# Small products of a one-block encoder: full-height filter products, f32r norm sums and first transform back, the low rank in one run, and GLA's values ahead of q and k

## The chip, the cores and the metric

The kernel runs on one core of a Trainium2 chip. The core has a matrix engine (TensorE, here PE), a vector engine (VectorE, DVE), a scalar engine (ScalarE, ACT), a general one (GpSimd, POOL), and SyncE (SP), which here issues DMAs; each executes its own instructions in order and waits for others on semaphores. The metric is the device time of one execution in microseconds, as the median of several. Lower is better.

## The reference

One encoder block on 256 rows of width 2048, in fp32. `w_in` projects the normed input to the operands of four mixers of width 512 each; their outputs go through `w_out`; cross attention over 256 memory rows and a SwiGLU follow.

```python
h = rms_norm(x, norm_g[l, 0])
q, k, v, g, lr, u_f, u_h, u_s = jnp.split(h @ w_in[l], split_at, axis=-1)
y_a = gla_mixer(q, k, v, g, lr, ...)        # gated linear attention, 4 heads, gates from lr (rank 2 x 16)
y_b = rms_norm(fnet_mixer(u_f), grp_norm_g[l, 0])
filt = hyena_filters(feats, w1, b1, w2, b2, w3, freq, decay)
y_c = rms_norm(hyena_mixer(u_h, hy_conv_w[l], filt, hy_skip[l]), grp_norm_g[l, 1])
y_d = rms_norm(shortconv_mixer(u_s, sc_conv_w[l]), grp_norm_g[l, 2])
x = x + concatenate([y_a, y_b, y_c, y_d]) @ w_out[l]
x = x + cross_attention(rms_norm(x, norm_g[l, 1]), mem_n, w_xq[l], w_xkv[l], w_xo[l])
x = x + swiglu(rms_norm(x, norm_g[l, 2]), w_gate_up[l], w_down[l])

def hyena_filters(...):      # an MLP of 64 over position features, twice sin, then:
    h = h @ w3               # 64 -> 2 orders x 2 directions x 512
    h = h * exp(-t * abs(decay))
    return rfft(two_sided(h))
def long_conv(z, filt, skip):
    return irfft(rfft(z, n=2 * seq) * filt)[:, :seq] + z * skip
def hyena_mixer(u, conv_w, filt, skip):
    v, x1, x2 = split(short_conv(u, conv_w))
    z = x1 * long_conv(v, filt[0], skip[0])
    return x2 * long_conv(z, filt[1], skip[1])
```

## The kernel before

**Large products.** All weights come as one stream of 128x128 blocks in the order of use. SP loads slabs of 16 blocks into three `raw` buffers (L83); ACT casts half a slab, eight blocks, to f32r (`wh`, L104) and DVE subtracts that from the original (`wl`, L105), two or three halves ahead of their use. Activations are split in the same way into slots of 128x512: 256 columns of high part, 256 of low. A product of two fp32 numbers is three f32r products. In `gemm` a block is the stationary operand: one matmul of `wh` with 512 columns (L301) and one of `wl` with 256 (L302), or three of 256 where it is `narrow` (L298, L299, L302). In `gemm_rows` the activations are stationary and four blocks pass through as 512 columns, three matmuls for each half of the rows (L346 to L348).

**Order.** The large products follow each other without a gap: keys (`w_xkv`, L301, from 5 us), the attention's values (L346 to L348, from 99 us), then `w_in`: Hyena's operands and GLA's k and q (L301, from 203 us), GLA's values (L346 to L348, from 303 us), the first three short convolution products and Fnet's (narrow, from 329 us), the other short convolution products (from 371 us), GLA's gate (narrow, from 443 us), then `w_out` (from 469 us) and what follows.

**Small work.** Generators in the class `Background` issue the small products, norms and transforms between those matmuls. `poll` lets a generator go on when the PE time counted since its last `yield` is over 1.3 us (or what the yield asks for) and little DVE work is owed. Tile's scheduling then sets the place within an engine's order. PE executes in order, so a small product whose operand is late holds up the large ones behind it.

**The places that the change touches.**

- `Hyena.filters`, L1033 and L1034: filters as `hs` (128 rows: 64 of the high part of the hidden layer, 64 of its low part) times `wh`, then the upper 64 rows times the upper 64 of `wl`. The weight rows are loaded twice, one copy above the other.
- `Hyena.dft`, L979 to L981: the transform forward, as three f32r products for each parity. `Hyena.convs`, L1100: the first transform back, two fp32 products for each parity from the table `tab`, which holds a factor of 1/256. L1119: the second transform back, also fp32.
- `rstd_bank`, L276 to L278: a diagonal of the reciprocal norms (DVE) times a matrix of ones (fp32), which spreads the norm of each row over all partitions; called once for the memory, once for x, for three group norms and for four GLA heads. `rstd_end` copies the result out (L283).
- `start_x`, L430 to L441: during the last value product it scales each of 16 tiles of x and splits it; after every fourth it issues four fp32 products of 32 columns each (L438), side by side in PE's columns, which add up to GLA's low rank `lr`.
- `Gla.open`: loads the gate weights `gkw` to a tile of their own.

Of the kernel before, what the change touches and what calls it, by code (L numbers as in the profile page):

```python
# [13 lines left out]
F32 = mybir.dt.float32  # L14
F32R = mybir.dt.float32r
# [22 lines left out]

ROWS = ((256, 512), (768, 832), (NBLK - 48 * FT, NBLK))

# [127 lines left out]
class Block:  # L168
# [99 lines left out]

    def rstd_bank(self, y, g=0):

        nc = self.nc
        dg = self.rp.tile([P, R], F32, name="dg", tag="dg", bufs=2)
        self.bg.dve(256, 2)
        for r in range(2):
            s = slice(r * P, (r + 1) * P)
            nc.vector.tensor_scalar(out=dg[:, s], in0=self.ident, scalar1=y[:, 2 * g + r:2 * g + r + 1], scalar2=None, op0=ALU.mult)  # L276
        p = self.bank()
        nc.tensor.matmul(p[:, 0:R], self.ones, dg, start=True, stop=True)  # L278
        return p[:, 0:R]

    def rstd_end(self, y, g=0, keep=None):
        rs = keep.tile([P, R], F32, name=f"krs{next(self.kept)}") if keep else self.rp.tile([P, R], F32, name="rs", tag="rs")
        self.nc.scalar.copy(rs, self.rstd_bank(y, g))  # L283
        return rs
# [85 lines left out]
    def run(self):  # L370
        nc, cp = self.nc, self.cp
        st = self.st
        self.act = [cp.tile([P, 512], F32R, name=f"act{i}") for i in range(24)]
        self.res = [cp.tile([P, 4, R], F32, name=f"res{i}") for i in range(4)]
        self.resk = lambda i: self.res[i // 4][:, i % 4, :]
        self.vec = cp.tile([P, NV], F32, name="vec")
        self.ones = cp.tile([P, P], F32, name="ones")
# [13 lines left out]

        self.load_x = lambda k, n: load("xT", k, n)

        nc.vector.memset(self.ones, 1.0)

        p = self.bank()
        for _ in range(10):
            nc.tensor.matmul(p[:, 0:P], self.ones, self.ones, start=True, stop=True)
        nc.vector.memset(self.eps, EPS)
# [14 lines left out]
    def mixers(self):  # L414
# [9 lines left out]

        low, lrp = [], []

        def start_x(n):

            x = self.tmp()
            self.stt(x, self.resk(n), self.gvec(V_NG, n), self.rsx, ALU.mult, ALU.mult)  # L430
            self.split(h[n], x)
            low.append(x)
            if n % 4 == 3:
                if n == 3:
                    lrp.append(self.bank()[:, 0:R])
                for g, x in enumerate(low):
                    k = n - 3 + g
                    nc.tensor.matmul(lrp[0][32 * g:32 * g + 32, :], gl.lrw[:, 32 * k:32 * k + 32], x, start=n == 3, stop=n == 15)  # L438
                low.clear()
                if n == 15:  # L440
                    nc.scalar.copy(gl.lr, lrp[0])  # L441

# [15 lines left out]
        def prepare(mid):  # L458
# [9 lines left out]
            col = self.rstd_cols(c[1][:, 0:2], D)  # L468
            yield
            self.rsx = self.rstd_end(col, 0, mid)  # L470

# [18 lines left out]

        with tc.tile_pool(name="mid", bufs=1) as mid:
            gl = Gla(self, mid)
            with tc.tile_pool(name="hyp", bufs=1) as hyp, tc.tile_pool(name="k2", bufs=8) as k2:
# [13 lines left out]
                for hd in range(4):  # L507
                    for r, p in enumerate(self.gemm_rows("w_xkv", [D + hd * 512], h, start_x if hd == 3 else None)[0]):
                        for c in range(2):
# [9 lines left out]

                self.gemm("w_in", [UH + i * P for i in range(12)], h, ev_u)  # L520
                self.gemm("w_in", [256, 384, 0, 128], h, lambda i, p: gl.feed(i, self.merge(p)))
                for r, p in enumerate(self.gemm_rows("w_in", [512], h)[0]):
                    nc.scalar.copy(gl.v[r], p)
                self.gemm("w_in", cols[0:NSC], h, ev_s, narrow=True)
# [369 lines left out]
class Hyena:  # L894
# [5 lines left out]
    def __init__(self, b, pool, k2):  # L900
        self.b, self.k2, self.ready, self.pending = b, k2, False, None
        tile_ = lambda n, s, dt=F32: pool.tile(s, dt, name=n)
        self.tab = tile_("tab", [P, 512])
        self.tabh, self.tabl = (tile_(n, [P, 512], F32R) for n in ("tabh", "tabl"))
        self.sp = [[[tile_(f"sp{o}{c}{k}", [P, 512]) for k in range(2)] for c in range(2)] for o in range(2)]
        self.x1 = tile_("x1", [P, 2, 512])
        self.x2 = [tile_(f"x2{i}", [P, R]) for i in range(4)]
        self.c33 = tile_("c33", [33, R + 64])
        self.w2 = tile_("w2", [64, 64])

# [41 lines left out]
    def sine(self, p, bias):  # L952
# [16 lines left out]
        return a  # L969

    def dft(self, cs, m, out):

        b, nc = self.b, self.b.nc
        ps = []
        for par in range(2):
            p = b.bank()
            o = slice((cs * 2 + par) * P, (cs * 2 + par + 1) * P)
            (hi, lo), th, tl = m[par], self.tabh[:, o], self.tabl[:, o]
            nc.tensor.matmul(p, th, hi, start=True, stop=False)  # L979
            nc.tensor.matmul(p, th, lo, start=False, stop=False)  # L980
            nc.tensor.matmul(p, tl, hi, start=False, stop=True)  # L981
            ps.append(p)
# [9 lines left out]
    def filters(self):  # L992
# [3 lines left out]
        nc.sync.dma_start(fwd, t["dft"][:, 0:512])  # L996
        nc.sync.dma_start(self.c33, t["c33"])
        nc.sync.dma_start(self.w2, t["c64"][0:64, 0:64])
        p = b.bank()
        nc.tensor.matmul(p[0:64, 0:R], self.c33[:, R:R + 64], self.c33[:, 0:R], start=True, stop=True)  # L1000
        h = self.sine(p[0:64, 0:R], V_B1)
        for _ in range(4):
            yield
        b.split2(self.tabh, self.tabl, fwd)
        yield
        p = b.bank()
        nc.tensor.matmul(p[0:64, 0:R], self.w2, h, start=True, stop=True)
        h = self.sine(p[0:64, 0:R], V_B2)
# [5 lines left out]
        for o in range(2):  # L1014
# [12 lines left out]
            for r in range(2):  # L1027
                hd = []
                for d in range(2):
# [3 lines left out]
                    nc.tensor.matmul(p, hs[:, s], wh, start=True, stop=False)  # L1033
                    nc.tensor.matmul(p, hs[0:64, s], wl[0:64, :], start=False, stop=True)  # L1034
                    win = self.piece()
# [27 lines left out]
    def spectrum(self, o):  # L1063
# [8 lines left out]
        for cs in range(2):  # L1072

            m = []
            for k in range(2):
                m0, m1 = self.piece(), self.piece()
                b.tt(m1, z[1][k], (hc if cs else hs)[k], ALU.mult)
                b.tt(m0, z[0][k], (hs if cs else hc)[k], ALU.mult)
                b.tt(m0, m0, m1, ALU.add if cs else ALU.subtract)
# [8 lines left out]
    def convs(self):  # L1088
# [3 lines left out]
        yield from self.spectrum(0)  # L1092
        yield
        while self.fed < 9:
            yield
        self.z = []
        for par in range(2):
            p = b.bank()
            for cs in range(2):
                nc.tensor.matmul(p, self.table(cs, par), self.y[cs][par], start=cs == 0, stop=cs == 1)  # L1100
            b.bg.pe(1.7)
            z = self.piece()
            b.tt(z, p, self.x1[:, par, :], ALU.mult)
            self.z.append(self.halves(z))
            yield SOON
        yield
        yield from self.spectrum(1)
        yield
        while self.fed < 12:
# [17 lines left out]
class Gla:  # L1127
# [12 lines left out]
    def open(self, pool):  # L1140
        nc, t = self.b.nc, self.b.t
        tile_ = lambda n, s, dt=F32: pool.tile(s, dt, name=n)
        self.w = [tile_(f"gw{i}", [P, 4, R]) for i in range(4)]
        self.gkw = tile_("gkw", [P, 512])
        self.msk = tile_("gmask", [P, R + P])
# [3 lines left out]
        self.ref = tile_("gref", [P, 3, 16])  # L1149
        self.gate = [tile_(f"gg{i}", [P, R]) for i in range(4)]  # L1150
        self.o = tile_("go", [P, 4, R])
# [189 lines left out]
def constants():  # L1341
# [4 lines left out]
    fwd = [fn(a) for fn in (np.cos, np.sin) for a in par]  # L1346
    dft = np.concatenate(fwd + [m.T / 256 for m in fwd], 1).astype(np.float32)

# [85 lines left out]
```

## Time and profile before

| | |
|---|---|
| median of 3 runs | 1498.02 us (1497.65 to 1498.56) |
| the profiled execution | 1498.32 us, span 1496.5 us |
| mean granted TensorE clock | 0.998 |
| PE busy of 60 to 350 us | 289.8 of 290 us |
| DVE busy of 275 to 330 us | 39.5 of 55 us |
| DVE, ACT busy of 350 to 470 us | 91.0, 71.3 of 120 us |
| L1034, 64 rows, x8 | 496 ns each, by L1033 (128 rows) 393 ns |
| L1100, fp32 passes of 512 columns, x8 | 592 ns each |
| L278, fp32 passes of 256 columns, x18 | 381 ns each |
| L438, fp32 passes of 32x256, x32 | 391 ns each |

The length of a matmul in the profile is its latency; matmuls overlap, so what one takes from the stream is the distance from its start to the next one's start. An fp32 product counts as two passes. The table of PE's waits says for how long PE stood still for another engine.

### The profile page before, as it was taken

The page shows a single profiled execution, that of the slowest core. Times are in us where ns is not written, and L with a number is a line of the kernel's source. Part 1 is how long each engine was busy: PE and PEld are TensorE (multiplying, and loading weights), DVE is VectorE, ACT ScalarE, POOL GpSimd, SP SyncE. Part 2 cuts the span into 40 slices and gives each one's busy share as a digit, 9 for nine tenths or more (in the row PEclk, how much of TensorE's full clock was granted, in tenths as well). Part 3 has the DMA queues.
Part 4 walks back from the last instruction along what each step waited for, and adds up shares of the span by engine and source line. Part 5 has one row for each costly group of instructions (what it writes and reads, how often), then busy time and mean ns, then how long its engine had stood idle before and what let it go on. Part 6 is the DMA issues. An engine that isn't in the chain of part 4 may idle for free.

```text
span 1496.5 us, 19811 instructions
## 1 busy us (share of the span) xinstructions
PE 1485.9 (99%) x7582; PEld 1254.2 (84%) x7582; DVE 938.3 (63%) x1373; ACT 759.3 (51%) x1125; POOL 149.7 (10%) x260
## 2 busy tenths in 40 slices
PE   9999999999999999999999999999999999999997
PEld 8887788889899888888888888888888888888886
DVE  6676778778777767877765554555554456444444
ACT  6565555557545655756544444444444445434344
POOL 0100100000000001200042401111110112000000
PEclk9999999999999999999999999999999999999999
DMA  9975554454546555554567756666666666555554
GB/s 355 347 250 193 189 192 160 167 192 142 183 142 222 188 185 201 193 179 152 189 194 253 239 207 213 216 223 225 209 204 211 220 222 226 185 186 194 197 196 141
DMA packets 56174, 306.11 MB, mean 205 GB/s; under 512 B 9197, under 2 KB 10510, under 8 KB 24464
## 3 DMA queue, kind: packets, MB, share of 16 engines
q1 hardware_dynamic: 45632, 281.11, 54.2%
q0 software_dynamic: 10016, 23.08, 4.9%
q8 instruction: 59, 0.97, 0.3%
q10 hardware_dynamic: 432, 0.66, 0.1%
q14 instruction: 35, 0.29, 0.1%
HBM read 291.18 MB, written 13.63 MB: 204 GB/s over the span
## 4 chain that ended last, share of the span: by engine, by line
PE 97%; ACT 1%; DVE 1%; DMA 0%; issue 0%; SPq 0%; ACTq 0%
PE pg L301 21%; PE pg L346 18%; PE pg L347 17%; PE pg L348 17%; PE pg L302 11%; PE pm L346 1%; PE pm L348 1%; PE pm L347 1%; PE pg L298 1%; PE pg L299 1%; PE pm L301 1%; PE pm L725 1%; PE pm L698 0%; PE pm L302 0%; DMA raw<-in_W 0%
## 5 line engine op out<-in xcount | busy, mean ns | idle before, releaser
L105 DVE TENSOR_TENSOR wl<-raw,wh 128x1024 fp32r<-128x1024 f32 (+1 forms) x503 | 611.6, 1217 | 481.5 <-ACT wh L104 477.1
L104 ACT CAST wh<-raw 128x1024 fp32r<-128x1024 f32 (+1 forms) x503 | 524.3, 1043 | 595.2 <-PE pg L348 396.3
L301 PE MATMUL pg<-act,wh 128*128 128x512 f32 x1296 | 457.7, 395 | 0.3 <-ACT wh L104 0.3
L302 PE MATMUL pg<-act,wl 128*128 128x256 f32 x1472 | 412.4, 280 | 0.2 <-DVE wl L105 0.2
L346 PE MATMUL pg<-wh,act 128*128 128x512 f32 x1008 | 397.1, 394 | 0.0
L347 PE MATMUL pg<-wl,act 128*128 128x512 f32 x1008 | 395.9, 393 | 0.0
L348 PE MATMUL pg<-wh,act 128*128 128x512 f32 x1008 | 392.9, 390 | 0.0
L301 PEld LDWEIGHTS pg<-act,wh 128*128 128x128 f32 x1296 | 243.6, 188 | 54.3 <-ACT wh L104 0.6
L302 PEld LDWEIGHTS pg<-act,wl 128*128 128x128 f32 x1472 | 276.8, 188 | 2.3 <-issue 1.2
L346 PEld LDWEIGHTS pg<-wh,act 128*128 128x128 f32 x1008 | 189.3, 188 | 45.8 <-issue 1.7
L348 PEld LDWEIGHTS pg<-wh,act 128*128 128x128 f32 x1008 | 189.3, 188 | 42.5
L347 PEld LDWEIGHTS pg<-wl,act 128*128 128x128 f32 x1008 | 189.5, 188 | 38.6
L767 POOL DMA_DIRECT2D hidden<-u x88 | 56.9, 654 | 312.1 <-DVE u L764 310.6
L298 PE MATMUL pg<-act,wh 128*128 128x256 f32 x176 | 50.6, 288 | 0.0
L299 PE MATMUL pg<-act,wh 128*128 128x256 f32 x176 | 49.3, 280 | 0.0
L346 PE MATMUL pg<-wh,f 128*128 128x512 f32 x120 | 47.3, 394 | 0.0
L348 PE MATMUL pg<-wh,f 128*128 128x512 f32 x120 | 47.0, 392 | 0.0
L347 PE MATMUL pg<-wl,f 128*128 128x512 f32 x120 | 46.6, 388 | 0.0
L811 POOL DMA_DIRECT2D xrows<-tmp x48 | 27.7, 584 | 130.1 <-DVE tmp L808 126.0
L196 DVE TENSOR_TENSOR tmp<-pg,tmp 128x256 f32<-128x256 f32 x86 | 35.9, 418 | 6.7 <-ACT tmp L308 4.5
L308 ACT COPY tmp<-pg 128x256 f32<-128x256 f32 x85 | 30.9, 365 | 10.9 <-PE pg L302 10.8
L298 PEld LDWEIGHTS pg<-act,wh 128*128 128x128 f32 x176 | 33.2, 188 | 0.2
(272 smaller groups left out, 1239.6 us busy)
## 6 DMA issues: line engine op xcount, KB each, us to landing
raw<-in_W SPq DMA_DIRECT2D x246, 1024.0 KB, 4.9
raw<-in_W SPq DMA_DIRECT2D x11, 512.0 KB, 7.5
hidden<-u POOLq DMA_DIRECT2D x88, 64.0 KB, 3.0
tmp<-hidden POOLq DMA_DIRECT2D x44, 128.0 KB, 4.0
res<-in_xT SPq DMA_DIRECT2D x8, 512.0 KB, 6.0
k<-in_mem SPq DMA_DIRECT2D x8, 256.0 KB, 7.8
k<-in_x SPq DMA_DIRECT2D x8, 256.0 KB, 8.4
keys<-tmp POOLq DMA_DIRECT2D x16, 128.0 KB, 5.8
```

The lines of the kernel that those rows point to most:

```text
L104: nc.scalar.copy(wh[:, a:b], r[:, a:b])
L105: nc.vector.tensor_tensor(out=wl[:, a:b], in0=r[:, a:b], in1=wh[:, a:b].bitcast(F32), op=ALU.subtract)
L196: self.nc.vector.tensor_tensor(out=out, in0=a, in1=b, op=op)
L298: self.nc.tensor.matmul(p[:, 0:R], wh, slot[:, 0:R], start=start, stop=False)
L299: self.nc.tensor.matmul(p[:, 0:R], wh, slot[:, R:512], start=False, stop=False)
L301: self.nc.tensor.matmul(p[:, :], wh, slot[:, :], start=start, stop=False)
L302: self.nc.tensor.matmul(p[:, 0:R], wl, slot[:, 0:R], start=False, stop=stop)
L308: self.nc.scalar.copy(t, p[:, R:512])
L346: self.nc.tensor.matmul(p[:, :], hi, wh, start=start, stop=False)
L347: self.nc.tensor.matmul(p[:, :], hi, wl, start=False, stop=False)
L348: self.nc.tensor.matmul(p[:, :], lo, wh, start=False, stop=stop)
L767: nc.gpsimd.dma_start(to[:, :, 32 * a:32 * a + 32], u[32 * a:32 * a + 32, :].rearrange("f (b t) -> f b t", t=32))
```

## The change

Five things, all in the mixers' stage (the first 470 us of the trace of before):

1. The second filter product takes all 128 rows of `hs` and `wl`.
2. The first transform back works on f32r halves like the forward one: `triple` issues three products for each table and operand. The table of the even parity is split into `backh` and `backl`; for the odd parity the forward table's halves serve. The factor of 1/256 moves from the table into the multiplication by the filters' spectrum.
3. `rstd_bank` makes the diagonal in two halves (ACT makes the high one, DVE the low one) and issues two f32r products; the norm of x stays one fp32 product (`whole`) and waits until the attention's value rows have begun.
4. The 16 products of the low rank are issued in one run, behind the first block row of GLA's values; x is scaled in place for it.
5. GLA's values come ahead of k and q in the weight stream, and the offsets in `ROWS` follow. `gkw` shares its space with the gates, `c33` and `w2` with a `k2` piece.

```diff
-ROWS = ((256, 512), (768, 832), (NBLK - 48 * FT, NBLK))
+ROWS = ((256, 512), (704, 768), (NBLK - 48 * FT, NBLK))
...
-    def rstd_bank(self, y, g=0):
+    def rstd_bank(self, y, g=0, whole=False):
...
-        dg = self.rp.tile([P, R], F32, name="dg", tag="dg", bufs=2)
-        self.bg.dve(256, 2)
+        if whole:
+            dg = self.dgp.tile([P, R], F32R, name="dgh", tag="dgh", bufs=2).bitcast(F32)
...
+            nc.tensor.matmul(p[:, 0:R], self.ones, dg, start=True, stop=True)
+            return p[:, 0:R]
+        dg = [self.dgp.tile([P, R], F32R, name=n, tag=n, bufs=2) for n in ("dgh", "dgl")]
         for r in range(2):
-            s = slice(r * P, (r + 1) * P)
-            nc.vector.tensor_scalar(out=dg[:, s], in0=self.ident, scalar1=y[:, 2 * g + r:2 * g + r + 1], scalar2=None, op0=ALU.mult)
+            s, c = slice(r * P, (r + 1) * P), y[:, 2 * g + r:2 * g + r + 1]
+            nc.scalar.activation(dg[0][:, s], self.ident, AF.Copy, scale=c)
+            self.stt(dg[1][:, s], self.ident, c, dg[0][:, s].bitcast(F32), ALU.mult, ALU.subtract)
         p = self.bank()
-        nc.tensor.matmul(p[:, 0:R], self.ones, dg, start=True, stop=True)
+        for d in dg:
+            nc.tensor.matmul(p[:, 0:R], self.onesr, d, start=d is dg[0], stop=d is dg[1])
         return p[:, 0:R]
...
-            x = self.tmp()
-            self.stt(x, self.resk(n), self.gvec(V_NG, n), self.rsx, ALU.mult, ALU.mult)
+            x = self.resk(n)
+            self.stt(x, x, self.gvec(V_NG, n), self.rsx, ALU.mult, ALU.mult)
             self.split(h[n], x)
-            low.append(x)
-            if n % 4 == 3:
...
+        def low_rank():
+            p = self.bank()[:, 0:R]
+            for k in range(KT):
+                g = 32 * (k % 4)
+                nc.tensor.matmul(p[g:g + 32, :], gl.lrw[:, 32 * k:32 * k + 32], self.resk(k), start=k < 4, stop=k >= KT - 4)
+            nc.scalar.copy(gl.lr, p)
+            self.bg.pe(2.3)
...
-            self.rsx = self.rstd_end(col, 0, mid)
+            while not rows:
+                yield SOON
+            self.rsx = self.rstd_end(col, 0, mid, True)
...
+                for r, p in enumerate(self.gemm_rows("w_in", [512], h, lambda k: k or low_rank())[0]):
+                    nc.scalar.copy(gl.v[r], p)
                 self.gemm("w_in", [256, 384, 0, 128], h, lambda i, p: gl.feed(i, self.merge(p)))
-                for r, p in enumerate(self.gemm_rows("w_in", [512], h)[0]):
-                    nc.scalar.copy(gl.v[r], p)
...
+    def triple(self, p, th, tl, hi, lo, start, stop):
+        for n, (a, b) in enumerate(((th, hi), (th, lo), (tl, hi))):
+            self.b.nc.tensor.matmul(p, a, b, start=start and n == 0, stop=stop and n == 2)
...
         b.split2(self.tabh, self.tabl, fwd)
         yield
+        for cs in range(2):
+            s = slice(cs * P, (cs + 1) * P)
+            b.split2(self.backh[:, s], self.backl[:, s], self.table(cs, 0))
+        yield
...
-                    nc.tensor.matmul(p, hs[0:64, s], wl[0:64, :], start=False, stop=True)
+                    nc.tensor.matmul(p, hs[:, s], wl, start=False, stop=True)
...
-                b.tt(m1, z[1][k], (hc if cs else hs)[k], ALU.mult)
-                b.tt(m0, z[0][k], (hs if cs else hc)[k], ALU.mult)
+                b.stt(m1, z[1][k], 1.0 / 256, (hc if cs else hs)[k], ALU.mult, ALU.mult)
+                b.stt(m0, z[0][k], 1.0 / 256, (hs if cs else hc)[k], ALU.mult, ALU.mult)
...
+        ps = []
+        for par in range(2):
+            y = [self.halves(self.y[cs][par]) for cs in range(2)]
+            yield
+            ps.append(b.bank())
+            for cs in range(2):
+                o = (2 * cs + 1) * P if par else cs * P
+                th, tl = (self.tabh, self.tabl) if par else (self.backh, self.backl)
+                self.triple(ps[par], th[:, o:o + P], tl[:, o:o + P], *y[cs], cs == 0, cs == 1)
+            b.bg.pe(1.4)
         for par in range(2):
-            p = b.bank()
-            for cs in range(2):
-                nc.tensor.matmul(p, self.table(cs, par), self.y[cs][par], start=cs == 0, stop=cs == 1)
-            b.bg.pe(1.7)
             z = self.piece()
-            b.tt(z, p, self.x1[:, par, :], ALU.mult)
+            b.tt(z, ps[par], self.x1[:, par, :], ALU.mult)
...
-        self.gate = [tile_(f"gg{i}", [P, R]) for i in range(4)]
+        gate = tile_("gg", [P, 4, R])
+        self.gate = [gate[:, i, :] for i in range(4)]
+        self.gkw = gate[:, 0:2, :].rearrange("p h r -> p (h r)")
...
-    dft = np.concatenate(fwd + [m.T / 256 for m in fwd], 1).astype(np.float32)
+    dft = np.concatenate(fwd + [m.T for m in fwd], 1).astype(np.float32)
```

More of the change, by code (lines that the diff above doesn't have):

```diff
@@ L267, in rstd_cols, with rstd_end @@
         return y
-    def rstd_bank(self, y, g=0):
+    def rstd_bank(self, y, g=0, whole=False):
         nc = self.nc
-        dg = self.rp.tile([P, R], F32, name="dg", tag="dg", bufs=2)
-        self.bg.dve(256, 2)
+        if whole:
+            dg = self.dgp.tile([P, R], F32R, name="dgh", tag="dgh", bufs=2).bitcast(F32)
+            self.bg.dve(256, 2)
+            for r in range(2):
+                s = slice(r * P, (r + 1) * P)
+                nc.vector.tensor_scalar(out=dg[:, s], in0=self.ident, scalar1=y[:, 2 * g + r:2 * g + r + 1], scalar2=None, op0=ALU.mult)
+            p = self.bank()
+            nc.tensor.matmul(p[:, 0:R], self.ones, dg, start=True, stop=True)
+            return p[:, 0:R]
+        dg = [self.dgp.tile([P, R], F32R, name=n, tag=n, bufs=2) for n in ("dgh", "dgl")]
         for r in range(2):
-            s = slice(r * P, (r + 1) * P)
-            nc.vector.tensor_scalar(out=dg[:, s], in0=self.ident, scalar1=y[:, 2 * g + r:2 * g + r + 1], scalar2=None, op0=ALU.mult)
+            s, c = slice(r * P, (r + 1) * P), y[:, 2 * g + r:2 * g + r + 1]
+            nc.scalar.activation(dg[0][:, s], self.ident, AF.Copy, scale=c)
+            self.stt(dg[1][:, s], self.ident, c, dg[0][:, s].bitcast(F32), ALU.mult, ALU.subtract)
         p = self.bank()
-        nc.tensor.matmul(p[:, 0:R], self.ones, dg, start=True, stop=True)
+        for d in dg:
+            nc.tensor.matmul(p[:, 0:R], self.onesr, d, start=d is dg[0], stop=d is dg[1])
         return p[:, 0:R]
-    def rstd_end(self, y, g=0, keep=None):
+    def rstd_end(self, y, g=0, keep=None, whole=False):
         rs = keep.tile([P, R], F32, name=f"krs{next(self.kept)}") if keep else self.rp.tile([P, R], F32, name="rs", tag="rs")
-        self.nc.scalar.copy(rs, self.rstd_bank(y, g))
+        self.nc.scalar.copy(rs, self.rstd_bank(y, g, whole))
         return rs
@@ L376, in run @@
         self.vec = cp.tile([P, NV], F32, name="vec")
-        self.ones = cp.tile([P, P], F32, name="ones")
+        self.onesr = cp.tile([P, P], F32R, name="ones")
+        self.ones = self.onesr.bitcast(F32)
         self.ident = cp.tile([P, P], F32, name="ident")
@@ L423, in start_m @@
                 self.split_scaled(h[n], self.resk(n), self.mg[:, n:n + 1])
-        low, lrp = [], []
+        rows = []
         def start_x(n):
-            x = self.tmp()
-            self.stt(x, self.resk(n), self.gvec(V_NG, n), self.rsx, ALU.mult, ALU.mult)
+            x = self.resk(n)
+            self.stt(x, x, self.gvec(V_NG, n), self.rsx, ALU.mult, ALU.mult)
             self.split(h[n], x)
-            low.append(x)
-            if n % 4 == 3:
[L434 to L441, printed above, removed]
+        def low_rank():
[5 more added lines that the diff above has]
+            self.bg.pe(2.3)
         def squares(src, c):
@@ L468, in prepare @@
             col = self.rstd_cols(c[1][:, 0:2], D)
-            yield
-            self.rsx = self.rstd_end(col, 0, mid)
+            while not rows:
+                yield SOON
+            self.rsx = self.rstd_end(col, 0, mid, True)
         UF, UH, US = 1568, 2080, 3616
@@ L491, in mixers @@
         with tc.tile_pool(name="mid", bufs=1) as mid:
+            self.dgp = mid
             gl = Gla(self, mid)
@@ L507, in mixers @@
                 for hd in range(4):
-                    for r, p in enumerate(self.gemm_rows("w_xkv", [D + hd * 512], h, start_x if hd == 3 else None)[0]):
+                    for r, p in enumerate(self.gemm_rows("w_xkv", [D + hd * 512], h, start_x if hd == 3 else rows.append)[0]):
                         for c in range(2):
@@ L904, in __init__ @@
         self.tabh, self.tabl = (tile_(n, [P, 512], F32R) for n in ("tabh", "tabl"))
+        self.backh, self.backl = (tile_(n, [P, 2 * P], F32R) for n in ("backh", "backl"))
         self.sp = [[[tile_(f"sp{o}{c}{k}", [P, 512]) for k in range(2)] for c in range(2)] for o in range(2)]
@@ L907, in __init__ @@
         self.x2 = [tile_(f"x2{i}", [P, R]) for i in range(4)]
-        self.c33 = tile_("c33", [33, R + 64])
-        self.w2 = tile_("w2", [64, 64])
     def piece(self):
@@ L978, in dft @@
             (hi, lo), th, tl = m[par], self.tabh[:, o], self.tabl[:, o]
-            nc.tensor.matmul(p, th, hi, start=True, stop=False)
-            nc.tensor.matmul(p, th, lo, start=False, stop=False)
-            nc.tensor.matmul(p, tl, hi, start=False, stop=True)
+            self.triple(p, th, tl, hi, lo, True, True)
             ps.append(p)
@@ L996, in filters @@
         nc.sync.dma_start(fwd, t["dft"][:, 0:512])
-        nc.sync.dma_start(self.c33, t["c33"])
-        nc.sync.dma_start(self.w2, t["c64"][0:64, 0:64])
+        small = self.piece()
+        c33, w2 = small[0:33, 0:R + 64], small[0:64, R + 64:R + 128]
+        nc.sync.dma_start(c33, t["c33"])
+        nc.sync.dma_start(w2, t["c64"][0:64, 0:64])
         p = b.bank()
-        nc.tensor.matmul(p[0:64, 0:R], self.c33[:, R:R + 64], self.c33[:, 0:R], start=True, stop=True)
+        nc.tensor.matmul(p[0:64, 0:R], c33[:, R:R + 64], c33[:, 0:R], start=True, stop=True)
         h = self.sine(p[0:64, 0:R], V_B1)
@@ L1005, in filters @@
         yield
+        for cs in range(2):
+            s = slice(cs * P, (cs + 1) * P)
+            b.split2(self.backh[:, s], self.backl[:, s], self.table(cs, 0))
+        yield
         p = b.bank()
-        nc.tensor.matmul(p[0:64, 0:R], self.w2, h, start=True, stop=True)
+        nc.tensor.matmul(p[0:64, 0:R], w2, h, start=True, stop=True)
         h = self.sine(p[0:64, 0:R], V_B2)
@@ L1092, in convs @@
         yield from self.spectrum(0)
-        yield
         while self.fed < 9:
             yield
+        ps = []
[8 more added lines that the diff above has]
+            b.bg.pe(1.4)
         self.z = []
         for par in range(2):
-            p = b.bank()
-            for cs in range(2):
-                nc.tensor.matmul(p, self.table(cs, par), self.y[cs][par], start=cs == 0, stop=cs == 1)
-            b.bg.pe(1.7)
             z = self.piece()
-            b.tt(z, p, self.x1[:, par, :], ALU.mult)
+            b.tt(z, ps[par], self.x1[:, par, :], ALU.mult)
             self.z.append(self.halves(z))
@@ L1107, in convs @@
         yield from self.spectrum(1)
-        yield
         while self.fed < 12:
@@ L1143, in open @@
         self.w = [tile_(f"gw{i}", [P, 4, R]) for i in range(4)]
-        self.gkw = tile_("gkw", [P, 512])
         self.msk = tile_("gmask", [P, R + P])
```

## The prediction

> **What bounds the kernel now.** First the page's table of engines (busy us, share of the span of 1496.5 us), then the chain that ended last, by engine.
>
> ```profile
> PE 1485.9 (99%) x7582; PEld 1254.2 (84%) x7582; DVE 938.3 (63%) x1373; ACT 759.3 (51%) x1125; POOL 149.7 (10%) x260
> ...
> PE 97%; ACT 1%; DVE 1%; DMA 0%; issue 0%; SPq 0%; ACTq 0%
> ```
>
> TensorE (PE) is the chain for 97% of the span. Busy PE time alone proves little, because matmuls overlap, so I asked PE's own waits: those on another engine come to 2.4 us in all, 1.1 of them in the warm-up before the first weight arrives.
>
> ```profile
> PE pm L398 <- DVE eps L399: 1.1, 1, 1.1
> ...
> PE pm L1007 <- ACT tmp L968: 0.2, 1, 0.2
> ```
>
> So what an edit is worth is the PE time between the last large-product matmul ahead of a small product and the first undisturbed one behind it. The timeline gives that from starts, and starts are what I use: the 0.39 us of a row is its latency. In the large products a 512-column f32r matmul starts 0.23 us after the one before it, a 256-column one takes 0.117 (L301 to L302 to L301: 0.23 + 0.12).
>
> ```profile
> 101.65 0.39 PE L348 MATMUL pg<-wh,act 128*128 128x512 f32 x1
> 101.88 0.39 PE L1033 MATMUL pm<-w3h,hs 128*128 128x512 f32 x1
> 102.20 0.50 PE L1034 MATMUL pm<-w3l,hs 64*128 64x512 f32 x1
> 102.63 0.50 PE L346 MATMUL pg<-wh,act 128*128 128x512 f32 x1
> 102.96 0.39 PE L347 MATMUL pg<-wl,act 128*128 128x512 f32 x1
> ```
>
> This is PE's timeline (start in us, length in us, line, tiles, shape, count) around one filter pair. The 64-row L1034 starts 0.32 after L1033 instead of 0.23, L346 0.43 after L1034, and L347 0.33 after that. Next, the forward transform:
>
> ```profile
> 125.97 0.39 PE L979 MATMUL pm<-w3h,tabh 128*128 128x512 f32 x1
> ...
> 127.33 0.39 PE L346 MATMUL pg<-wh,act 128*128 128x512 f32 x1
> ```
>
> Six full f32r products (L979 to L981 twice) take 1.36, nothing lost. Then a block of the low rank, and the fp32 products of the first transform back:
>
> ```profile
> 182.85 0.40 PE L348 MATMUL pg<-wh,act 128*128 128x512 f32 x1
> 183.17 0.64 PE L438 MATMUL pm<-tmp,gv 128*32 128x256 f32 x8
> 183.74 0.50 PE L346 MATMUL pg<-wh,act 128*128 128x512 f32 x1
> 184.08 0.39 PE L347 MATMUL pg<-wl,act 128*128 128x512 f32 x1
> ```
>
> ```profile
> 279.31 0.28 PE L302 MATMUL pg<-act,wl 128*128 128x256 f32 x1
> 279.43 1.88 PE L1100 MATMUL pm<-k,tab 128*128 128x512 f32 x4
> 280.75 0.80 PE L301 MATMUL pg<-act,wh 128*128 128x512 f32 x1
> 281.38 0.28 PE L302 MATMUL pg<-act,wl 128*128 128x256 f32 x1
> ```
>
> An fp32 product is two passes (L1100 x4 is two products), each 0.43 where an f32r one of the same width takes 0.23.
>
> **The change part by part.** All prices are PE time.
>
> *Filters.* From L348 to L347 is 1.31; without the pair it would be 2 x 0.23 = 0.46, so a pair costs 0.85 (0.87 in the second order, from 142 us). Eight pairs: 6.9. Afterwards both products are full height, as L979 to L981 are: 8 x 0.46 = 3.7. **-3.2.** Ends: 0, if the loss is not the height's, to -3.2.
>
> *First transform back.* From L302 at 279.31 to L302 at 281.38 is 2.07, less 0.35 for one plain pair of matmuls: 1.72; the second parity (283.5) costs the same: 3.44 for four fp32 products. Afterwards twelve f32r products in two groups of six like L979's, 1.39 each (the dearer of those groups): 2.8. **-0.7.** They need four splits more: 4 casts of 0.617 (L212) and 4 subtractions of 0.685 (L196, w3l). The code issues these one yield, at least 1.3 us of PE work, ahead of the products; from 275 to 330 us DVE is busy 39.5 of 55 us and ACT 29.8, so they fit beside the large products. If the cover were gone, one cast and one subtraction would show for each parity, 2 x 1.3 = 2.6. The 1/256 that moves from the table into the spectrum turns 16 tensor_tensor of 0.684 into scalar_tensor_tensor of 0.687 (L200 on 512): nothing. The two 256-wide splits of the table (2 x 0.40 ACT, 2 x 0.42 DVE) stand behind the tabh split in the filters' chain, ahead of L1007, whose wait of 0.2 they can lengthen by at most 0.8.
>
> *Norms.* At 64 us L302 stands at 64.03 and again at 64.82: 0.79 - 0.35 = 0.44 for one fp32 spreading product (L278 x2). Two f32r ones of 256 columns take 2 x 0.117 = 0.235, as in the narrow products (L298, L299). Of nine calls eight change (memory, three group norms, four GLA heads); the ninth, `whole`, stays fp32 and only moves behind the first value rows. 8 x 0.2 = **-1.6.**
>
> *Low rank.* From L348 at 182.85 to L347 at 184.08 is 1.23, less 0.46: 0.77 for a block of four, 3.1 for four blocks. In a block four 32-column products lie side by side, so it is two passes of 0.215 (0.43 for L278's two) and 0.34 of entering and leaving. In one run that 0.34 is paid once: 8 x 0.215 + 0.34 = 2.06. Ends 2.06 and 3.1; in the trace the second pass on the same 32 columns starts 0.24 after the first (183.17, 183.41), so it is nearest to the low end: 8 x 0.24 + 0.3 = 2.2. **-0.9.** The in-place stt replaces one of the same size.
>
> *Order.* GLA's values ahead of q and k, the ROWS offsets, gkw inside the gates, c33 and w2 in a k2 piece: the same matmuls, loads and casts in another order; PE has no wait now at either border of the value rows. Nothing. The piece with c33 and w2 is one of eight and is held until L1007 (76 us); on SP's queue the next k2 loads behind the x rows were issued from 81 us, later than that, so no weight load gets stuck behind them.
>
> *New waits.* A spreading sum now needs ACT (a scaled 128-wide copy, twice) and then DVE, where two DVE scalings of 0.28 did. No row shows a scaled 128-wide copy; a plain one is 0.26 (L212, 128 wide), a scaled 256-wide one 0.51 (L546), so 0.26 to 0.51, and I take 0.36. Mostly there is room: dg is ready 16.5 us ahead of L278 at 64, 3.5 at 342, 25 at 429. Between 446 and 466 us there is not:
>
> ```profile
> 446.77 0.47 DVE L276 TENSOR_SCALAR dg<-ident,rc 128x128 f32<-128x128 f32 x2
> ...
> 448.25 1.02 PE L278 MATMUL pm<-dg,ones 128*128 128x256 f32 x4
> ```
>
> There the lead is 1.0 us. In the built order the eight copies for the heads stand on ACT between Squares, weight casts of 1.05, the table load of 1.28 and the gates' Silu. The fourth head's second copy is behind two casts and its last product a dozen matmuls later; the shortconv norm's second copy is behind a Silu and a cast, then DVE has a 1.22 subtraction (L105) first. Behind a waiting sum PE holds the whole gate product. I expect three brushes (fourth head, shortconv norm, first split of w_out behind it) of 0.1 to 0.3: **+0.4.** Ends 0 and 2.3 (one cast and one subtraction at one of them).
>
> Sum: -3.2 - 0.7 - 1.6 - 0.9 + 0.4 = -6.0. The profiled execution took 1498.32 us (span 1496.5 and 1.8 around it), 0.3 above the median of 1498.02: profiled about 1492.3, median 1492.0. A measurement of this kernel tells about 0.2% (3.0 us) from no change, so 1495.0 is the border.
>
> **Rivals.**
>
> *The loss is not the height's.* If the 0.4 us of a filter pair came with the operands (another bank, a late w3l) and not with 64 rows, full height would pay it too: 1492.0 + 3.2 = 1495.2, no change. Against it: L980 reads w3l without any loss. The Trainium skill says the same as this rival from another side: "TensorE: Matmul & The Clock Gate", section "Why this matters for your kernels", has a single 32-row matmul take as long as a 128-row one, by which the filters' edit gains nothing; "TensorEngine Tiling", section "Key Properties", has every change of tiling mode drain the array. This case's trace sides with the second: 0.09 lost ahead of L1034 and 0.3 behind it. 4%.
>
> *The sums wait.* Every one of the five sums between 446 and 466 us stands behind one cast and one subtraction (1.05 + 1.22 less the lead of 1.0): 5 x 1.3 = 6.5 in place of 0.4, 1498.1, no change. For it: ACT's order above. Against it: ACT is busy 71.3 of 120 us from 350 to 470, and the products were placed later where the operand is late. Half of it (1495) is likelier than all. 5%.
>
> *Slower.* The weight stream starves in that stretch: ACT executes in order, so a weight cast put behind a Silu or a copy that waits for PE is late, its subtraction too, and PE runs dry one half slab later. A half is eight blocks, 8 x 0.35 = 2.8 us of PE. It decides when a cast is late by more than the halves held ahead (two, 5.6 us); if the four casts of the gate product each lost a half, 4 x 2.8 = 11.2 more: 1503. For it: the cast that now stands behind the first gate's Silu started 2.4 us ahead of that Silu (449.95, 452.31). Against it: 2.4 is under 5.6, and PE's waits on L104 and L105 are 0.7 us in the whole run. 2%.
>
> **How the numbers follow.** Forecast 89%, with the rivals at 4, 5 and 2%. Range: low end with all waits at 0 and the low rank at 2.06 (-6.6), less 0.5 for the scatter of the runs: 1490.9; high end 1495.0, which takes in the low rank at 3.1 (+0.9) and the waits at 2.3 (+1.9) together, and the near half of the second rival. Faster by over 0.2%: 0.89 and a part of the second rival, 0.91; same 0.07; slower 0.02.
>
> **What would show it.** In the profile after: a filter pair that costs 0.46; six L987 in place of L1100 x4 twice, 1.39 each; each spreading sum as two starts 0.12 apart; one run of the low rank of about 2.2; PE's waits still under 4 us, the new ones between 440 and 465. Wrong would be: filter starts still 0.32 and 0.43 apart, a PE wait on dgh or dgl over 1 us, or waits on wh or wl there.

## The result and the profile after

The changed kernel takes 1492.36 us (median of 6, 1491.72 to 1493.07) against 1497.98 us before (median of 6, 1497.57 to 1498.56): a ratio of 0.9962, 95% interval 0.9949 to 0.9975. That is 5.6 us less, where 6.0 had been forecast. The profiled execution took 1492.38 us, its span is 1490.6, 5.9 under the span before. The granted clock is 0.998 or 0.999 in every execution compared here; one of the ten of `e3`, at 0.752, took 1831.41 us and stands in no ratio. The page's engine table and the chain:

```profile
PE 1479.3 (99%) x7586; PEld 1254.6 (84%) x7586; DVE 942.3 (63%) x1379; ACT 767.6 (51%) x1147; POOL 150.1 (10%) x260
...
PE 96%; ACT 1%; DVE 1%; DMA 0%; issue 0%; SPq 0%; ACTq 0%
```

PE still carries the span, with 6.6 us less busy time, and 4 and 8 us more work on DVE and ACT. PE's waits, all of them (engine, line, engine and line waited for: us in total, times, longest):

```profile
PE pm L409 <- DVE eps L410: 1.1, 1, 1.1
PE pg L311 <- ACT wh L104: 0.9, 2, 0.6
PE pm L1029 <- ACT tmp L981: 0.3, 1, 0.3
PE pm L312 <- DVE wl L105: 0.2, 1, 0.2
PE pg L312 <- DVE wl L105: 0.2, 1, 0.2
PE pg L311 <- DVE act L196: 0.2, 1, 0.2
```

They sum to 2.9 us (2.4 before). The last is new: the first split of `w_out`. The 0.4 of L1319 (Fnet, waiting for ACT's copy `fu`) is no longer listed; by the starts that place, now L1347, loses 0.40 where it lost 0.70. In the code after, the large products' lines are L308 to L312 and L356 to L358, the filters' L1055 and L1056, the transforms' L987, the sums' L288 (f32r) and L279 (fp32), the low rank's L449. PE's timeline (start, length, line, tiles, shape, count) at the filters:

```profile
107.34 0.40 PE L358 MATMUL pg<-wh,act 128*128 128x512 f32 x1
107.58 0.39 PE L1055 MATMUL pm<-w3h,hs 128*128 128x512 f32 x1
107.81 0.40 PE L1056 MATMUL pm<-w3l,hs 128*128 128x512 f32 x1
108.04 0.39 PE L356 MATMUL pg<-wh,act 128*128 128x512 f32 x1
108.27 0.39 PE L357 MATMUL pg<-wl,act 128*128 128x512 f32 x1
```

Four steps of 0.23 or 0.24, nothing lost: a pair is 0.93 - 0.46 = 0.47. The low rank, then the first parity of the first transform back:

```profile
268.85 0.39 PE L358 MATMUL pg<-wh,act 128*128 128x512 f32 x1
269.17 1.93 PE L449 MATMUL pm<-res,gv 128*32 128x256 f32 x32
271.04 0.51 PE L356 MATMUL pg<-wh,act 128*128 128x512 f32 x1
271.38 0.40 PE L357 MATMUL pg<-wl,act 128*128 128x512 f32 x1
...
273.68 0.40 PE L358 MATMUL pg<-wh,act 128*128 128x512 f32 x1
273.92 0.39 PE L987 MATMUL pm<-w3h,backh 128*128 128x512 f32 x1
...
275.31 0.39 PE L356 MATMUL pg<-wh,act 128*128 128x512 f32 x1
```

The low rank is 2.53 - 0.46 = 2.07 in one piece; a parity is 1.63 - 0.23 = 1.40. Last, the sum at 64 us, and the place behind the last norm where PE now stands still:

```profile
63.87 0.28 PE L312 MATMUL pg<-act,wl 128*128 128x256 f32 x1
63.98 0.28 PE L288 MATMUL pm<-dgh,ones 128*128 128x256 f32 x1
64.10 0.28 PE L288 MATMUL pm<-dgl,ones 128*128 128x256 f32 x1
64.22 0.39 PE L311 MATMUL pg<-act,wh 128*128 128x512 f32 x1
64.45 0.28 PE L312 MATMUL pg<-act,wl 128*128 128x256 f32 x1
...
463.62 0.40 PE L311 MATMUL pg<-act,wh 128*128 128x512 f32 x1
464.20 0.50 PE L311 MATMUL pg<-act,wh 128*128 128x512 f32 x1 [0.18 <-DVE act L196]
464.54 0.28 PE L312 MATMUL pg<-act,wl 128*128 128x256 f32 x1
```

A sum is 0.58 - 0.35 = 0.23 where it was 0.44. At 464 us the distances are 0.58 and 0.34 where 0.23 each would be free: 0.46 lost. In the trace of before the same place lost 0.09, 0.32 between these two starts:

```profile
469.96 0.48 PE L301 MATMUL pg<-act,wh 128*128 128x512 f32 x1
470.28 0.28 PE L302 MATMUL pg<-act,wl 128*128 128x256 f32 x1
```

The other sum that waits is the fourth head's (after; the first row is still the third head's):

```profile
448.09 0.28 PE L288 MATMUL pm<-dgl,ones 128*128 128x256 f32 x1
448.29 0.38 PE L288 MATMUL pm<-dgh,ones 128*128 128x256 f32 x1
448.51 0.28 PE L308 MATMUL pg<-act,wh 128*128 128x256 f32 x1
...
449.94 0.28 PE L308 MATMUL pg<-act,wh 128*128 128x256 f32 x1
450.07 0.39 PE L288 MATMUL pm<-dgl,ones 128*128 128x256 f32 x1
450.29 0.28 PE L309 MATMUL pg<-act,wh 128*128 128x256 f32 x1
```

The distances are 0.20 and 0.22, then 0.13 and 0.22, where 0.12 each would be free: 0.30 lost.

### The profile page after: what moved, and what is told of

It is laid out like the page before. It is cut to its first block, busy times and chain, and to the rows that moved or that the text cites. A ratio compares the mean times of both kernels' runs of the same rounds, so it can differ in the third digit from the quotient of the medians.

```text
span 1490.6 us, 19837 instructions
## 1 busy us (share of the span) xinstructions
PE 1479.3 (99%) x7586; PEld 1254.6 (84%) x7586; DVE 942.3 (63%) x1379; ACT 767.6 (51%) x1147; POOL 150.1 (10%) x260
## 4 chain that ended last, share of the span: by engine, by line
PE 96%; ACT 1%; DVE 1%; DMA 0%; issue 0%; SPq 0%; ACTq 0%
PE pg L311 21%; PE pg L357 17%; PE pg L358 17%; PE pg L356 17%; PE pg L312 11%; PE pm L357 1%; PE pm L356 1%; PE pm L358 1%; PE pm L987 1%; PE pm L311 1%; PE pg L308 1%; PE pg L309 1%; PE pm L738 1%; PE pm L711 0%; PE pm L312 0%; DMA raw<-in_W 0%
## 5 line engine op out<-in xcount | busy, mean ns | idle before, releaser
L105 DVE TENSOR_TENSOR wl<-raw,wh 128x1024 fp32r<-128x1024 f32 (+1 forms) x503 | 611.8, 1218 | 476.8 <-ACT wh L104 470.1
L104 ACT CAST wh<-raw 128x1024 fp32r<-128x1024 f32 (+1 forms) x503 | 525.1, 1045 | 584.2 <-PE pg L358 397.9
L312 PE MATMUL pg<-act,wl 128*128 128x256 f32 x1472 | 412.2, 280 | 0.2 <-DVE wl L105 0.2
L358 PE MATMUL pg<-wh,act 128*128 128x512 f32 x1008 | 396.1, 393 | 0.0
L357 PE MATMUL pg<-wl,act 128*128 128x512 f32 x1008 | 395.7, 393 | 0.0
L356 PE MATMUL pg<-wh,act 128*128 128x512 f32 x1008 | 392.7, 390 | 0.0
L312 PEld LDWEIGHTS pg<-act,wl 128*128 128x128 f32 x1472 | 276.8, 188 | 1.5 <-DVE wl L105 0.5
L356 PEld LDWEIGHTS pg<-wh,act 128*128 128x128 f32 x1008 | 189.2, 188 | 43.5 <-issue 0.4
L357 PEld LDWEIGHTS pg<-wl,act 128*128 128x128 f32 x1008 | 189.3, 188 | 42.6
L358 PEld LDWEIGHTS pg<-wh,act 128*128 128x128 f32 x1008 | 189.4, 188 | 38.7
L308 PE MATMUL pg<-act,wh 128*128 128x256 f32 x176 | 50.0, 284 | 0.0
L357 PE MATMUL pg<-wl,f 128*128 128x512 f32 x120 | 47.3, 394 | 0.0
L356 PE MATMUL pg<-wh,f 128*128 128x512 f32 x120 | 47.0, 392 | 0.0
L358 PE MATMUL pg<-wh,f 128*128 128x512 f32 x120 | 46.6, 388 | 0.0
L308 PEld LDWEIGHTS pg<-act,wh 128*128 128x128 f32 x176 | 33.3, 189 | 0.1
```

Source lines behind the costliest of these rows:

```text
L104: nc.scalar.copy(wh[:, a:b], r[:, a:b])
L105: nc.vector.tensor_tensor(out=wl[:, a:b], in0=r[:, a:b], in1=wh[:, a:b].bitcast(F32), op=ALU.subtract)
L308: self.nc.tensor.matmul(p[:, 0:R], wh, slot[:, 0:R], start=start, stop=False)
L312: self.nc.tensor.matmul(p[:, 0:R], wl, slot[:, 0:R], start=False, stop=stop)
L356: self.nc.tensor.matmul(p[:, :], hi, wh, start=start, stop=False)
L357: self.nc.tensor.matmul(p[:, :], hi, wl, start=False, stop=False)
```

## The experiments

Eleven runs, in three groups, each beside the kernel before on its own chip (1497.69, 1497.75 and 1498.01 us in the three). Medians of one program scatter by some 0.5 us between groups, so terms under 1 us are read from PE's starts.

**The filters undone** (`e1_half_filters`), in the changed kernel:

```diff
-nc.tensor.matmul(p, hs[:, s], wl, start=False, stop=True)
+nc.tensor.matmul(p, hs[0:64, s], wl[0:64, :], start=False, stop=True)
```

> The changed kernel with the second filter product back on 64 rows. Theory (the height costs): starts 0.32, 0.43 and 0.33 us apart again, a pair 0.86 instead of 0.47, 8 x 0.39 = 3.1 us more: 1492.4 + 3.1 = 1495.5. Rival (the loss came with the operands, their place or a late split, which are now others): pairs stay at 0.47, time at 1492.4.

1495.24 us, ratio 0.9983 (0.9974 to 0.9992). The second pair, with the weight loads of its matmuls (PEld; rows between left out):

```profile
108.17 0.19 PEld L1055 LDWEIGHTS pm<-w3h,hs 128*128 128x128 f32 x1
108.40 0.39 PE L1055 MATMUL pm<-w3h,hs 128*128 128x512 f32 x1
...
108.72 0.18 PEld L1056 LDWEIGHTS pm<-w3l,hs 64*128 64x128 f32 x1 [0.35 <-issue]
108.72 0.50 PE L1056 MATMUL pm<-w3l,hs 64*128 64x512 f32 x1
109.15 0.19 PEld L356 LDWEIGHTS pg<-wh,act 128*128 128x128 f32 x1 [0.25 <-issue]
109.15 0.50 PE L356 MATMUL pg<-wh,act 128*128 128x512 f32 x1
```

The pair is back at 0.86, the time 2.9 up (3.1 by the ratios, since the kernel before was faster in this group too): the height costs, in the same place and with the same operands. The rows also say how. The load for L1055 starts 0.23 ahead of its matmul, while the one before still streams. The loads for L1056 and for L356 behind it start only with their matmuls. So at each change between 128 and 64 rows the overlap of load and stream is lost.

**The filters alone** (`e2_filters_only`): the same line changed the other way, in the kernel before.

> The kernel before with only the filters' second product on 128 rows. Theory: the edit stands alone, pairs fall from 0.86 to 0.47, 1498.0 - 3.1 = 1494.9. Rival (the pairs became cheap because of what else moved): 1498.0, pairs at 0.86.

1494.66 us, ratio 0.9978 (0.9969 to 0.9987), pairs of 0.46 and 0.48: 3.0 us, the edit stands alone.

**Both filter products on 64 rows** (`e3_both_half`):

```diff
-nc.tensor.matmul(p, hs[:, s], wh, start=True, stop=False)
-nc.tensor.matmul(p, hs[:, s], wl, start=False, stop=True)
+nc.tensor.matmul(p, hs[0:64, s], wh[0:64, :], start=True, stop=False)
+nc.tensor.matmul(p, hs[0:64, s], wl[0:64, :], start=False, stop=True)
```

> The changed kernel with both filter products on 64 rows; the low part of the hidden layer is left out of the filters. Theory (going between 128 and 64 rows costs, 0.1 on the way in and 0.3 on the way out): the second product starts 0.23 after the first, the way in and out is paid once, a pair costs 0.86 as with one short product, 1495.5. Rival (a 64-row product is slow by itself, 0.43 each): the second starts 0.43 after the first, a pair costs about 1.05, 1492.4 + 8 x 0.58 = 1497.0.

1495.46 us, ratio 0.9982 (0.9973 to 0.9992).

```profile
106.98 0.40 PE L358 MATMUL pg<-wh,act 128*128 128x512 f32 x1
107.30 0.18 PEld L1055 LDWEIGHTS pm<-w3h,hs 64*128 64x128 f32 x1 [0.36 <-issue]
107.31 0.49 PE L1055 MATMUL pm<-w3h,hs 64*128 64x512 f32 x1
107.41 0.19 PEld L1056 LDWEIGHTS pm<-w3l,hs 64*128 64x128 f32 x1
...
107.64 0.39 PE L1056 MATMUL pm<-w3l,hs 64*128 64x512 f32 x1
107.96 0.19 PEld L356 LDWEIGHTS pg<-wh,act 128*128 128x128 f32 x1 [0.36 <-issue]
107.96 0.51 PE L356 MATMUL pg<-wh,act 128*128 128x512 f32 x1
...
108.31 0.40 PE L357 MATMUL pg<-wl,act 128*128 128x512 f32 x1
```

From L358 to L357 is 1.33, a pair 0.87: two short products cost no more than one, so it is the change of height that is paid for, once on the way in and once on the way out. The detail expected was off: the second starts 0.33 after the first. Between the two the load is ahead again (107.41, 0.23 before its matmul); the extra 0.1 is L1055's own load, which came late. By these rows, then, a change costs about 0.1 before its load and 0.1 for the load itself, seen in the distance behind it: 2 x 0.2 = 0.4.

**The low rank in four blocks** (`e4_lowrank_four`), behind the first four block rows of GLA's values:

```diff
-            for k in range(KT):
+            for k in range(4 * n, 4 * n + 4):
...
-self.gemm_rows("w_in", [512], h, lambda k: k or low_rank())
+self.gemm_rows("w_in", [512], h, lambda k: k < 4 and low_rank(k))
```

> The changed kernel with the low rank in four blocks of four products again, behind the first four block rows of GLA's values. Theory (0.34 of entering and leaving is paid once for a run): four blocks of 0.77 in the profile, 3 x 0.34 = 1.0 us more, 1493.4. Rival (the run got cheaper for its place or for reading x in place): four blocks of about 0.52, 1492.4.

1493.50 us, ratio 0.9968 (0.9955 to 0.9980). The blocks cost 0.77, 0.77, 0.78 and 0.77, in all 3.09 against 2.07: 1.0 more, as the theory has it, in the new place and with x read in place. The time rose by 1.1 (L1347's wait, below, is 0.3 longer here).

**Both halves of the sums' diagonal on DVE** (`e5_sums_on_dve`):

```diff
-nc.scalar.activation(dg[0][:, s], self.ident, AF.Copy, scale=c)
+nc.vector.tensor_scalar(out=dg[0][:, s], in0=self.ident, scalar1=c, scalar2=None, op0=ALU.mult)
+self.bg.dve(128)
```

> The changed kernel with both halves of the norms' diagonal made on DVE (a scaling to f32r, then the subtraction), so that no spreading sum waits for ACT. Theory (the waits of 0.2 and 0.1 at the fourth head, and 0.26 at the first split of w_out, come from the copies queued on ACT): they go, 1492.4 - 0.5 = 1491.9. Rival (DVE's own queue is as long there: four more scalings of 0.28 behind casts' subtractions of 1.22): the waits move to DVE, 0.4 at the heads and more at the last norm, 1492.4 to 1493.4.

1493.23 us, ratio 0.9971 (0.9960 to 0.9982), 0.9 worse than the changed kernel. The waits move as the rival has it: `w_out`'s is gone, but the sums wait for DVE instead, at the heads and at the last norm:

```profile
443.53 0.28 PE L309 MATMUL pg<-act,wh 128*128 128x256 f32 x1
444.05 0.39 PE L289 MATMUL pm<-dgl,ones 128*128 128x256 f32 x1 [0.24 <-DVE dgl L200]
...
462.83 0.28 PE L289 MATMUL pm<-dgh,ones 128*128 128x256 f32 x1
463.30 0.39 PE L289 MATMUL pm<-dgl,ones 128*128 128x256 f32 x1 [0.19 <-DVE dgl L200]
```

Both second products start 0.5 after the matmul before them, where 0.12 is free. By the starts the heads lose 0.54 more than in the changed kernel and the last norm 0.45, `w_out` 0.46 less: 0.5 in all. The rest lies outside the sums, and what moved it was not looked into: Fnet's wait for `fu` (L1348 here) is 0.6 longer, a forward transform at 227 us takes 0.3 more, and the first 14 us are 0.6 shorter.

**GLA's values behind k and q again** (`e6_old_order`), the low rank as one run ahead of k:

> The changed kernel with GLA's values behind k and q again, the low rank as one run ahead of k. Theory (the order is worth nothing): 1492.4, within 0.3. Rival (the order hides the first transform back, whose splits would be late in the k and q products): waits on PE at the first transform back, up to 2 x 1.3, 1493 to 1495.

1491.47 us, ratio 0.9958 (0.9945 to 0.9971): not slower, if anything faster (0.9 by the medians, 0.6 by the ratios). The first transform back is 1.39 for each parity here too, without a wait, so the rival falls. Where it differs is Fnet's L1347 (L1348 here): its second eight passes and the matmul behind cost 1.73 in this kernel and 2.13 in the changed one. There ACT puts two gate activations of 1.05 each (L1241, L1244) and three weight casts between its two copies of `fu` (L544), and the second copy starts 0.7 after the first of the eight passes; here only three casts lie between, and it starts 1.0 ahead of them. That is 0.4; most of the rest lies in the first 14 us (below).

**The first transform back as fp32** (`e7_back_fp32`), with the 1/256 left where the change puts it and without the four splits ahead of the products:

```diff
-self.triple(ps[par], th[:, o:o + P], tl[:, o:o + P], *y[cs], cs == 0, cs == 1)
+nc.tensor.matmul(ps[par], self.table(cs, par), self.y[cs][par], start=cs == 0, stop=cs == 1)
```

> The changed kernel with the first transform back as fp32 products again. Theory (1.72 against 1.39 for each parity): 2 x 0.33 = 0.7 more, 1493.1. Rival (what the four splits cost on ACT and DVE delays the weights' casts, which eats the gain): 1492.4 or less.

1492.83 us, ratio 0.9967 (0.9954 to 0.9980). The parities cost 1.71 and 1.72, so 0.65 of PE time as expected. What followed shifted: Hyena's norm came earlier against ACT's queue and waited,

```profile
333.82 0.28 PE L309 MATMUL pg<-act,wh 128*128 128x256 f32 x1
334.56 0.39 PE L288 MATMUL pm<-dgh,ones 128*128 128x256 f32 x1 [0.46 <-ACT dgh L284]
```

0.74 where 0.12 is free, and L1347's wait is 0 here. Neither lies in the transform's own products.

**All sums as fp32** (`e8_sums_fp32`):

```diff
-        if whole:
+        if True:
```

> The changed kernel with every spreading sum as one fp32 product of a diagonal from DVE. Theory (0.44 against 0.235 for each of eight, 1.6 in all, of which 0.3 was lost to the waits on ACT and 0.3 to the later first split of w_out): 1492.4 + 1.6 - 0.6 = 1493.4. Rival (f32r is worth nothing net, the waits eat all of it): 1492.4.

1492.51 us, ratio 0.9967 (0.9955 to 0.9980): by the medians no difference from the changed kernel. By the starts: eight sums cost 3.46 against 2.21, but `w_out` loses 0.09 in place of 0.46 and L1029 0.12 less. 1.25 - 0.37 - 0.12 = 0.8 net of f32r, half of its 1.6. L1029 is the filters' second hidden product, which needs the sine of the first (L1018). From L1018 to L1029 pass 6.23 us in this kernel, in the changed one and in the kernel before. But here and in the kernel before, L1018 stands one 256-column product earlier in PE's order, so PE has 0.12 more of work with which to fill those 6.23 us.

**The changed kernel again** (`a1_changed_again`), beside the next two:

> The changed kernel once more, on the chip and beside the kernels that it is compared with here: 1492.4, all terms as in its first profile. Open: the wait of L1347 for ACT's copy of fu (0.4 in that profile, 0 with the old order) and the first 14 us of the run, which differed by 0.5 between executions of kernels that are alike there.

1491.80 us, ratio 0.9959 (0.9945 to 0.9973). All terms are the same to 0.02, L1347's too (2.11). But the first norm sum starts at 63.37 us here and at 63.98 in the first profile, by the same instructions in the same order: PE's waits for the first weights (L104) are 0.2 here and 0.9 there.

**Sums by place** (`e9_sums_by_place`): the old order, x's sum f32r, the shortconv norm's sum fp32.

> The kernel with the old order, and the sums chosen by place: x's norm, which has time, as f32r too, the shortconv norm, behind which the first split of w_out is late, as one fp32 product. Theory (a sum is worth 0.2 where ACT has time, and loses 0.36 at w_out where it hasn't): 0.2 less for x, 0.2 more for the shortconv norm's product, 0.36 less for w_out's wait: 0.36 under the old-order kernel, 1491.1. Rival (the wait at w_out comes with the stretch's other copies, not with that norm's): 1491.5, the wait stays.

1491.66 us, ratio 0.9959 (0.9947 to 0.9972): no difference in the medians. The starts show what was expected of x (0.44 to 0.24) and most of what was expected of `w_out` (0.17 lost where 0.46 was), at 0.2 more for the norm's sum: 0.3 net, below what medians tell. So 0.29 of that wait goes with the shortconv norm's f32r sum.

**The hidden products on full height and width** (`e10_full_mlp`), on top of that:

```diff
+nc.gpsimd.memset(small[:, 0:R + 192], 0.0)
...
-nc.tensor.matmul(p[0:64, 0:R], c33[:, R:R + 64], c33[:, 0:R], start=True, stop=True)
+nc.tensor.matmul(p[:, 0:R], small[:, R:R + P], small[:, 0:R], start=True, stop=True)
...
-nc.tensor.matmul(p[0:64, 0:R], w2, h, start=True, stop=True)
+nc.tensor.matmul(p[:, 0:R], small[:, R + 64:R + 192], h, start=True, stop=True)
```

> The kernel with sums by place, and the filters' two hidden products (33 and 64 rows by 64 columns) on all 128 rows and columns, padded with zeros. Theory (leaving the full size costs, as at the filters): each falls from 0.77 to the 0.44 of a full fp32 product of 256 columns, 0.33 each, 1491.1 - 0.7 = 1490.4, if the second's operand isn't late by as much. Rival (the sine chain behind the first product sets the second's start, so its wait takes what is saved): the first's 0.33 comes back as a longer wait of the second, 1490.8 to 1491.1.

1491.26 us, ratio 0.9956 (0.9944 to 0.9969), the lowest median of all, though the changed kernel's ratio lies in its interval. The first product fell from 0.77 to 0.44. The second, from 1.15 to 0.87: it still waits for its sine.

```profile
75.10 0.39 PE L311 MATMUL pg<-act,wh 128*128 128x512 f32 x1
75.66 0.70 PE L1030 MATMUL pm<-tmp,k 128*128 128x256 f32 x2 [0.17 <-ACT tmp L982]
```

The first product bears the theory out, and the same rule found a place that the change had left. The second's 0.28 can't be put down to its height alone: in this kernel ACT loads the sine's table ahead of the end of DVE's work for it and not behind, so 5.28 us pass between the two products where 6.23 passed in `e9`, and PE's wait is 0.14 shorter. Against the kernel before it is 6.75 us (1498.01 in this group).

## Why the prediction was right

Step by step, against its terms:

- *Filters, -3.2.* Measured -3.1: eight pairs from 6.9 to 3.8. Undone it costs 2.9 (`e1`), alone it brings 3.0 (`e2`). The first rival falls with `e1`: same operands, half height, loss back. Of the two sections of the Trainium skill that were set against each other, "Key Properties" in "TensorEngine Tiling (Array Packing)" (a change of tiling mode drains the array) is the one that the runs bear out, with 0.2 us for each change of height; that the array drains is not to be seen in these traces, the late weight load is. The other's single short product taking as long as a full one is not contradicted by `e3`, where both are short and lose only at the borders; it leaves the borders out.
- *First transform back, -0.7.* Measured -0.65. The cover held: no wait on the splits in any profile, in either order.
- *Low rank, -0.9.* Measured -1.0, the low end: 2.06 had been reckoned for a run with one way in and out, 2.07 was found. The 0.24 taken for each pass was too careful: the run's eight passes take 1.93, of which the last 0.38 is latency, so they lie (1.93 - 0.38) / 7 = 0.22 apart on average.
- *Norms, -1.6, and new waits, +0.4.* The sums alone gave -1.57. Two of the three expected waits came: 0.30 at the fourth head, 0.37 more at `w_out`'s first split; none at the shortconv norm's own sum. With 0.12 at L1029 that is +0.8, so this term was mis-sized by 0.4: the split of `w_out`, two steps behind the norm's sum, lost more than the 0.1 to 0.3 allowed for each brush, and L1029 was in no term. What the prediction had priced there (at most 0.8 for the splits of the table, taken as 256 wide) came to nothing: they are 128 wide, 0.30 on ACT and 0.29 on DVE each, and L1018 to L1029 takes 6.23 us before and after. The 0.12 comes with L1018's place in PE's order (`e8`). A scaled copy of 128 columns on ACT takes 0.40 (L284), where 0.36 had been taken. The Trainium skill's line for an ACTIVATE with one per-partition operand ("ScalarE: Activation LUTs", section "What ACT_TABLE_LOAD costs": 280 ns and 0.833 ns for each column) would have been an estimate of 0.39, which the trace bears out.
- *Order, 0.* The order by itself showed no gain (`e6`).

The terms make -3.1 - 0.65 - 1.0 - 1.6 + 0.8 = -5.6; L1347's shorter wait (0.3 less than before) brings -5.9, the spans' difference. No term held that wait, so that the sum of -6.0 was met this closely is luck by those 0.3; the medians say -5.6 here and -6.2 in the group of `a1`. The second rival came true for one of its five places, the fourth head, and 0.3 of its 6.5 us; its lead of 1.0 was that of the first two heads, while the trace of before has 2.9 for the other two and 3.2 for the norm. The third did not come true at all: PE's waits on L104 and L105 are 1.3 us, all of it in the first 14 us of the run.

## What to carry to other kernels

Where one engine is the chain from end to end, price an edit by the distance between the starts of undisturbed instructions around it, not by the lengths of its rows; four terms of under 4 us each came out to within 0.15 that way. In a stream of full-size matmuls, what is expensive about a small one is the way in and out: fill it up to full height or put small ones of a kind together, and look for the remaining ones, as `e10` did. A faster instruction that needs a further engine's queue ahead of it is worth its saving only where that queue has room: choose by place.

## What the runs showed of the hardware

A change between 128-row and 64-row products costs about 0.2 us of PE each way, about 0.1 until the weight load may start and 0.1 for its lost overlap, and two short products in a row pay no more than one (0.87 against 0.86). The waits of small products for ACT float: Fnet's wait for one copy was 1.0 (`e5`), 0.7 (before), 0.4 (the changed kernel) and 0 us (`e6`) in kernels whose Fnet code is the same, by what ACT had ahead of that copy; differences of that size say nothing about an edit elsewhere.
